# A two-layer decoder trunk: the four-expert round moved from last to fourth, with the overflow branches, two weight tiles and the last rows' parts re-ordered around it

## The chip, the cores and the metric

One core of a Trainium2 chip runs the whole kernel. The metric is device microseconds of one execution. Matmuls run on TensorE (PE, with its weight loads PEld); VectorE is DVE, ScalarE is ACT, GpSimd is POOL, and SyncE (SP) issues nearly all DMAs.

## What is computed

Two layers (DEPTH 2) over 256 tokens of 1024 columns. Each layer is a token mixer (four causal branches behind one input projection), a layer norm, then a mixture of 16 experts of which each token uses two, and a second layer norm:

```python
mix = token_mixer(x, cos, sin, lam_init, w_in[l], ...)
x = layer_norm(DEEPNORM_ALPHA * x + mix, ln1_g[l], ln1_b[l])
ffn = hierarchical_moe(x, w_rg[l], b_rg[l], w_re[l], b_re[l], w_gate[l], w_up[l], w_down[l])
x = layer_norm(DEEPNORM_ALPHA * x + ffn, ln2_g[l], ln2_b[l])
...
hg = jnp.einsum('bsd,edh->bseh', x, w_gate)
hu = jnp.einsum('bsd,edh->bseh', x, w_up)
act = jax.nn.silu(hg) * hu * gate[..., None]
return jnp.einsum('bseh,ehd->bsd', act, w_down)
```

`gate` is zero for the experts that a token does not use. The expert hidden size is 256, everything is float32.

## The kernel before, in words

**Weights come in units of 1 MB** (128 x 2048 float32). A layer has 33 units for the mixer and 48 for the experts: each expert has two units for gate and up (one for each half of the 1024 input columns) and one for down. SP issues one DMA for a unit (`Unit`, L117) as soon as the buffer that it goes to is free; `look(n)` (L448) issues units up to the n-th, in the order of the list `feed`, and `raw(e, j)` (L470) calls it each time that PE code asks for a unit, so the place of a DMA in SP's program follows the PE code with a lead. There are 14 rotating buffers (4 `raw`, 10 `sp`, `CYCLE`) and three more for the first units of the experts: a tile of two (`T16a`, units 8 and 9) and `acc` (unit 10). Below, "unit 38" is the 38th of the 48 in the order of `feed`, counted from 0; 48 to 51 are the first four of the next layer's mixer.

**The experts run in rounds.** A round multiplies the rows of a few experts at once, each in its own strip of PE: six rounds of two experts with 64 slots each, and one round of four experts with 32 slots. Rounds 0 to 2 are experts 0 to 5; the other ten are sorted by their number of tokens at run time, and the four smallest make the four-expert round, which is the last, round 6. In a round p PE does, one after the other and interleaved with the rounds beside it: `gu(p, 0)` and `gu(p, 1)` (L699, gate and up), `turn` (L738, L740, transposes), `down` (L707) and `scatter` (L715, the rows are added to their tokens in PSUM). `residual_mm` (L726) adds the layer's input, whose two parts `hl` ACT and DVE make (`residual_parts`, L719, L720). Matmuls go in order, so a unit that is late stops PE.

**Three branches on the numbers of tokens** stand in the expert part. `most` (L797): if the largest expert has over 64 tokens, three units of it are fetched again (`fetch`, L693, tiles `ow`, `od`) for its overflow. `past` (L852) takes the same condition and computes that overflow beside the last rounds. `rare` (L807): if more than that is needed, a long body with loops. In this run the largest expert has over 64 tokens in layer 1 and not in layer 0, and `rare` is never taken. Each engine has the branches in its own program, SP too, so a DMA that stands behind `rare` there waits until SP is past it. `spare` (L681 on) makes the overflow's slots on DVE and ACT.

**Around them**: the layer norm's rows `gb2` (tile `lnp`, 1 MB, L815) are loaded near the end of the experts; the small rows of the mixer `rw` (L1095) and `bc` (L1096) are loaded once per layer; `ahead` (L845) casts the first units of the next layer's mixer into high and low parts (ACT L134, DVE L138), and `parts_of` splits the last round's rows `y` in the same way (ACT L96, DVE L97) before their scatter.

Of the kernel before, what the change touches and what calls it, by code (L numbers as in the profile page):

```python
# [22 lines left out]
P = 128  # L23
# [12 lines left out]
STAT = 6  # L36
PAIRS = 6
HALF = CAP // 2
NP = PAIRS + 1
SLOTS = NP * 128  # L40
# [29 lines left out]
def trunk(ctx: ExitStack, tc: tile.TileContext, x, xT, wu, rows, brow, lnp, cst, ut, out):  # L70
# [40 lines left out]
    class Unit:  # L111


        def __init__(self, l, i, pieces=1, raw=None, src=None):
            self.raw = raw if raw is not None else raw_p.tile([P, 2048], F32, tag="raw", name=nm("raw"))
            if pieces:
                self.load = nc.sync.dma_start(self.raw, wu[l * NU + i] if src is None else src)  # L117
            self.parts = {}
            self.after = None

# [296 lines left out]
    def tail(l, x_in, mhi, mlo, rw, wg, sw, unit, last):  # L417
# [16 lines left out]
        def places(p):  # L434

            w = CAP if p < PAIRS else HALF
            c, c0 = (0, p * P) if p < STAT // 2 else (1, (p - STAT // 2) * P)
            return [(2 * p + j, slice(j * w, (j + 1) * w), xg[c], slice(c0 + j * w, c0 + (j + 1) * w)) for j in range(P // w)]

        def places_n(p):  # L440
            return [2 * p + j for j in range(2 if p < PAIRS else 4)] if 0 <= p < NP else []

# [5 lines left out]
        def look(n):  # L448
            while len(us) < min(n, limit if place else feed.index((STAT, 0))):
                i = len(us)  # L450
                if i >= len(feed):
                    us.append(Unit(l + 1, i - len(feed), raw=None if i == len(feed) else
                                   sp_p.tile([P, 2048], F32, tag="sp", name=nm("wr"))))
                else:
                    if i == 8:
                        two.append(mp.tile([P, 4096], F32, tag="T16a", name=nm("w2")))
                    if i in (8, 9):
                        r = two[0][:, (i - 8) * 2048:(i - 7) * 2048]
                    elif i == 10:
                        r = big.tile([P, 2048], F32, tag="acc", name=nm("w1"))  # L460
                    else:
                        r = None if (i if i < 8 else i - FIRST) % CYCLE in range(RAW) else sp_p.tile([P, 2048], F32, tag="sp", name=nm("wr"))
                    e, j = feed[i]
                    us.append(Unit(l, FIRST_E + 3 * e + j, raw=r) if e < STAT else Unit(l, None, raw=r, src=place[0](e + 4, j)))
# [59 lines left out]
        def gather(c, k, t, parts=(0, 1)):  # L524
# [24 lines left out]
        with manual():  # L549
# [68 lines left out]
            key = sm.tile([P, 16], F32, tag="key", name=nm("key"))  # L618
            top = sm.tile([P, 20], F32, tag="top", name=nm("top"))
            topi = sm.tile([P, 20], I32, tag="topi", name=nm("topi"))  # L620
            ei = sm.tile([P, 20], I32, tag="ei", name=nm("ei"))

            def counts():

                V.scalar_tensor_tensor(key, cn, 16.0, down15, op0=OP.mult, op1=OP.add)
                V.max(top[:, 10:18], key[:, STAT:])
# [3 lines left out]
                V.tensor_scalar(top[:, 16:20], low[:, 10:14], -1.0, None, op0=OP.mult)  # L630
                V.max(top[:, 0:8], key)
                V.scalar_tensor_tensor(top[:, 8:9], top[:, 0:1], -16.0 * MORE, top[:, 1:2], op0=OP.add, op1=OP.max)
                V.scalar_tensor_tensor(top[:, 8:9], top[:, 19:20], 16.0 * (CAP - HALF), top[:, 8:9], op0=OP.add, op1=OP.max)
                V.tensor_copy(top[:, 9:10], top[:, 8:9])
# [15 lines left out]
            def slot_gates(p0, p1):  # L650
                gp = psumd()[:, :(p1 - p0) * 8].rearrange("p (a b) -> p a b", b=8)
                for p in range(p0, p1):
                    n = len(places_n(p))
                    for t in range(2):
                        T.matmul(gp[:, p - p0, :2 * n], Q[t][:, p * P:(p + 1) * P],
                                 rts[t].gh[:, 2 * p:2 * p + n, :].rearrange("p a b -> p (a b)"), start=(t == 0), stop=(t == 1))
                for a, b, n in ((p0, min(p1, PAIRS), 2), (max(p0, PAIRS), p1, 4)):
                    for j in range(n if a < b else 0):
                        r = slice(j * P // n, (j + 1) * P // n)
                        V.tensor_reduce(gs[r, a:b], gp[r, a - p0:b - p0, 2 * j:2 * j + 2], axis=AX.X, op=OP.add)  # L660

            def order():
# [5 lines left out]
                for t in range(2):  # L668
                    o = sm.tile([P, 2, n], F32, tag="ord", name=nm("ord"))
                    for i, v in enumerate((rts[t].s16, rts[t].g16)):  # L670
                        V.tensor_tensor(m[:, 1], m[:, 0], v[:, None, :].to_broadcast([P, n, 16]), op=OP.mult)
                        V.tensor_reduce(o[:, i], m[:, 1], axis=AX.X, op=OP.add)
                    slots(t, STAT * CAP, o[:, 0, :2 * PAIRS - STAT])
                    slots(t, 2 * PAIRS * CAP, o[:, 0, 2 * PAIRS - STAT:], HALF)
                    finish(rts[t].two(slice(STAT, NE), o[:, 1]))
# [19 lines left out]
            def gu(p, kh, ps):  # L695
                w = [raw(i, kh) for i in places_n(p)]
                for k in range(4):
                    for (_, r, x_, c), w_ in zip(places(p), w):
                        T.matmul(ps[r, :], x_[:, 4 * kh + k, c], w_[:, k * 512:(k + 1) * 512],  # L699
                                 start=(kh == 0 and k == 0), stop=(kh == 1 and k == 3))  # L700

            def down(p, aT, pd, halves=(0, 1)):
                w = [raw(i, 2) for i in places_n(p)]
                for half in halves:
                    for k in range(2):
                        for (_, r, _, _), w_ in zip(places(p), w):
                            T.matmul(pd[half][r, :], aT[:, k, r], w_[:, k * 1024 + half * 512:k * 1024 + (half + 1) * 512],  # L707
# [49 lines left out]
            gu(0, 1, ps)  # L757
            slot_gates(0, STAT // 2)
            si = expert_act(ps, gs[:, 0:1])
# [10 lines left out]
            def pair(p, si, todo, ps=None):  # L770
# [9 lines left out]
                if p == 1:  # L780
                    slot_gates(STAT // 2, NP)
# [4 lines left out]
            for p in range(1, NP - 4):  # L786
                si, todo = pair(p, si, todo)
                if p == 1:
# [63 lines left out]
        with tc.If(most > 16 * CAP + 15, label=f"past{l}") as c:  # L852
            with manual():
                steps.chunk(0, CAP, (lambda: out6(0), lambda: out6(1), lambda: scatter6(0),
                                     lambda: (scatter6(1), turn7()), lambda: (ahead(0), down7((0,)))))
                ahead(1)
                down7((1,))
        with c.Else(), manual():
# [5 lines left out]
            ahead(0)  # L864
            ahead(1)
            down7()
        with manual():
            if last:
                A.activation(gs[:, 0:1], gs[:, 0:1], AF.Square)
            ahead(2)  # L870
            y = mp.tile([P, 2, D], F32, tag="T16a", name=nm("y"))
            y7 = big.tile([P, 2, 2, 512], F32R, tag="xtok", name=nm("y7"))
            yy = [parts_of((ps, tp6)[half], y7[:, half]) for half in range(2)]

# [67 lines left out]
            else:  # L942
# [9 lines left out]
                for half in range(2):  # L952
                    done(1, half)
                nc.sync.dma_start(x2d, y)
        return None if last else (x2d, nhi, nlo, us[len(feed):])

    def overflow(topi, counts, spare, fetch, ww, wd, oo, q, gt, x1, sums):
# [96 lines left out]
        def fours(i):  # L1054

            k_ = nc.values_load(topi[0:1, i:i + 1], min_val=0, max_val=16 * S + 15)
            with tc.If(k_ > 16 * HALF + 15):
                with manual():
                    fetch(i, ww, wd)
                    chunk(i, HALF)  # L1060
                if i > 16:
                    fours(i - 1)

        def rare():

            past(counts[0], 0, CAP + MORE)
            experts(1)
            fours(19)
            with manual():
                spare(0, CAP, q, gt)  # L1070
                fetch(0, ww, wd)

        return SimpleNamespace(chunk=chunk, rare=rare, room=room)

    def layer(l, x_in, thi, tlo, last, early):
# [3 lines left out]
        def unit():  # L1079
# [4 lines left out]
            return Unit(l, i)  # L1084

        lam_init = 0.8 - 0.6 * math.exp(-0.3 * l)
        tks = [slice(0, P), slice(P, 2 * P)]
# [394 lines left out]
```

## Time and profile before

| | |
|---|---|
| median of 3 runs | 687.53 us (686.36 to 689.56) |
| the profiled execution | 687.56 us |
| its span, first to last instruction | 685.8 us |
| mean granted TensorE clock | 0.986 |
| PE busy | 652.8 us (95%) |
| DVE, ACT busy | 412.3 us (60%), 287.0 us (42%) |
| DMA bytes | 185.73 MB, mean 271 GB/s |

The profiled execution stands 0.03 us from the median, and 1.8 us of it lie outside the span. Times in the trace count from the span's start. Layer 0 ends near 342 us, where PE takes up layer 1's input projection; the expert part of layer 1 lies about 335 us behind that of layer 0.

### The profile page before, as it was taken

The page shows a single profiled execution, that of the slowest core. Times are in us where ns is not written, and L with a number is a line of the kernel's source. Part 1 is how long each engine was busy: PE and PEld are TensorE (multiplying, and loading weights), DVE is VectorE, ACT ScalarE, POOL GpSimd, SP SyncE. Part 2 cuts the span into 40 slices and gives each one's busy share as a digit, 9 for nine tenths or more (in the row PEclk, how much of TensorE's full clock was granted, in tenths as well). Part 3 has the DMA queues.
Part 4 walks back from the last instruction along what each step waited for, and adds up shares of the span by engine and source line. Part 5 has one row for each costly group of instructions (what it writes and reads, how often), then busy time and mean ns, then how long its engine had stood idle before and what let it go on. Part 6 is the DMA issues. An engine that isn't in the chain of part 4 may idle for free. (4 is left out here: it accounts for less than half of the span.)

```text
span 685.8 us, 9776 instructions
## 1 busy us (share of the span) xinstructions
PE 652.8 (95%) x3579; PEld 462.3 (67%) x3579; DVE 412.3 (60%) x932; ACT 287.0 (42%) x465; POOL 5.9 (1%) x26
## 2 busy tenths in 40 slices
PE   8999999999999999998699999999999999999983
PEld 5899778888888354333479987888887953543331
DVE  4998667876557832211799875786853677321116
ACT  5755675454224231111455547664441252211122
POOL 0100000000000000000000000000000000000000
PEclk9999999999999999999899999999999999999997
DMA  8995544466759997979927363456566799699871
GB/s 302 369 338 190 206 131 176 172 219 224 289 192 391 410 419 290 396 291 424 421 100 275 123 236 105 152 183 249 182 225 265 271 409 421 261 402 418 318 326 62
DMA packets 28001, 185.73 MB, mean 271 GB/s; under 512 B 3104, under 2 KB 3232, under 8 KB 6432
## 3 DMA queue, kind: packets, MB, share of 16 engines
q1 hardware_dynamic: 27936, 184.94, 70.4%
q8 instruction: 32, 0.52, 0.3%
q14 instruction: 33, 0.27, 0.1%
HBM read 182.83 MB, written 2.10 MB: 270 GB/s over the span
## 5 line engine op out<-in xcount | busy, mean ns | idle before, releaser
L138 DVE TENSOR_TENSOR sp<-raw,sp 128x1024 fp32r<-128x1024 f32 x122 | 147.9, 1221 | 53.7 <-ACT sp L134 43.6
L134 ACT CAST sp<-raw 128x1024 fp32r<-128x1024 f32 x122 | 126.0, 1051 | 105.3 <-PE mm L229 72.5
L229 PE MATMUL mm<-sp,thi 128*128 128x512 f32 (+1 forms) x320 | 96.5, 382 | 1.5 <-ACT sp L96 0.9
L229 PE MATMUL mm<-sp,nhi 128*128 128x512 f32 (+1 forms) x320 | 97.4, 382 | 0.3 <-ACT nhi L96 0.3
L699 PE MATMUL ps<-wr,xg 128*64 128x512 f32 (+1 forms) x352 | 80.0, 596 | 0.0
L229 PEld LDWEIGHTS mm<-sp,thi 128*128 128x128 f32 x320 | 58.9, 188 | 13.5 <-ACT sp L96 1.5
L229 PEld LDWEIGHTS mm<-sp,nhi 128*128 128x128 f32 x320 | 58.8, 188 | 11.7 <-issue 0.5
L229 PE MATMUL mm<-sp,nlo 128*128 128x512 f32 (+1 forms) x160 | 61.4, 385 | 0.5 <-DVE nlo L97 0.4
L229 PE MATMUL mm<-sp,tlo 128*128 128x512 f32 (+1 forms) x160 | 60.1, 380 | 0.0
L699 PEld LDWEIGHTS ps<-wr,xg 128*64 128x64 f32 (+1 forms) x352 | 23.0, 128 | 37.2 <-issue 36.5
L229 PE MATMUL dn<-sp,yhl 128*128 128x512 f32 x192 | 47.8, 392 | 0.0
L409 DVE SCALAR_TENSOR_TENSOR si<-ps,gs,si 128x256 f32<-128x256 f32 x14 | 6.8, 483 | 62.6 <-ACT si L408 62.4
L699 PE MATMUL ps<-raw,xg 128*64 128x512 f32 (+1 forms) x144 | 43.2, 596 | 0.8 <-DVE xg L541 0.8
L229 PE MATMUL mm<-sp,mhl 128*128 128x512 f32 (+1 forms) x192 | 41.0, 368 | 0.9 <-ACT mhl L96 0.5
L229 PEld LDWEIGHTS dn<-sp,yhl 128*128 128x128 f32 x192 | 35.8, 188 | 7.4
L229 PEld LDWEIGHTS mm<-sp,mhl 128*128 128x128 f32 x192 | 32.6, 189 | 7.5 <-DVE mhl L97 1.1
L229 PE MATMUL mm<-thi,sp 128*128 128x256 f32 x192 | 35.6, 286 | 1.4 <-ACT scr L1225 1.3
L229 PE MATMUL mm<-nhi,sp 128*128 128x256 f32 x192 | 35.7, 286 | 0.3 <-ACT misc L1122 0.3
L97 DVE TENSOR_TENSOR yy<-dn,yy 128x512 fp32r<-128x512 f32 x24 | 16.4, 690 | 31.8 <-ACT yy L96 31.8
L229 PEld LDWEIGHTS mm<-sp,nlo 128*128 128x128 f32 x160 | 30.1, 188 | 6.6 <-DVE nlo L97 1.0
L229 PEld LDWEIGHTS mm<-sp,tlo 128*128 128x128 f32 x160 | 30.1, 188 | 5.5
L707 PE MATMUL dn<-wr,aT 128*64 128x512 f32 x112 | 31.5, 613 | 2.2 <-DMA wr<-in_wu_dram 2.2
(305 smaller groups left out, 974.8 us busy)
## 6 DMA issues: line engine op xcount, KB each, us to landing
raw<-in_wu_dram SPq DMA_DIRECT2D x91, 1024.0 KB, 5.2
wr<-in_wu_dram SPq DMA_DIRECT2D x63, 1024.0 KB, 9.5
w<-in_wu_dram SPq DMA_DIRECT2D x6, 1024.0 KB, 14.9
raw<-in_wu_dram SPq DMA_DIRECT2D x8, 256.0 KB, 6.0
lnp<-in_lnp_dram SPq DMA_DIRECT2D x4, 512.0 KB, 6.0
lnp<-in_lnp_dram SPq DMA_DIRECT2D x2, 1024.0 KB, 15.7
ow<-in_wu_dram SPq DMA_DIRECT2D x2, 1024.0 KB, 10.6
xr<-in_xT_dram SPq DMA_DIRECT2D x4, 256.0 KB, 5.8
```

Of the source, the lines that this page charges most:

```text
L97: eng.tensor_tensor(lo, src, f32(hi), op=OP.subtract)
L134: A.copy(self.parts[q][0], self.raw[:, q * 1024:(q + 1) * 1024])
L138: V.tensor_tensor(lo, self.raw[:, q * 1024:(q + 1) * 1024], f32(hi), op=OP.subtract)
L229: T.matmul(ps, a, b, start=(first and i == 0), stop=(last and i == n - 1))
L409: V.scalar_tensor_tensor(si, ps[:, 256:512], gate, si, op0=OP.mult, op1=OP.mult)
L699: T.matmul(ps[r, :], x_[:, 4 * kh + k, c], w_[:, k * 512:(k + 1) * 512], start=(kh == 0 and k == 0), stop=(kh == 1 and k == 3))
L707: T.matmul(pd[half][r, :], aT[:, k, r], w_[:, k * 1024 + half * 512:k * 1024 + (half + 1) * 512], start=(k == 0), stop=(k == 1))
```

## The change

- The four-expert round becomes round 3 (`FOUR`), right behind the three rounds of experts 0 to 5; rounds 4 to 6 are pairs again. `feed`, the sort's columns and the slots follow.
- `rare` is moved ahead of `pair(3)`, with `most` and its `fetch` and `spare` directly behind it. Before, `most` stood there and `rare` one round later.
- The early tile of two units is `T16b` in place of `T16a`, and holds units 6 and 7 in place of 8 and 9; the gathered rows `xg` and the overflow's `ow` change tiles accordingly.
- Layer 1's `rw` and `bc` are issued behind unit 37 of layer 0's experts; before, `bc` was issued early in the kernel and `rw` at the gather.
- `gb2` stands behind units 48 to 51 in SP's program; before, ahead of them.
- In the tail of layer 0, `ahead` casts one half of a unit ahead of `down7`, and the parts of the rows `y` then alternate with the next casts; before, three casts came first.

```diff
-PAIRS = 6
+FOUR = STAT // 2
 HALF = CAP // 2
-NP = PAIRS + 1
+NP = 7
...
-            w = CAP if p < PAIRS else HALF
+            w = HALF if p == FOUR else CAP
...
-                    if i == 8:
-                        two.append(mp.tile([P, 4096], F32, tag="T16a", name=nm("w2")))
-                    if i in (8, 9):
-                        r = two[0][:, (i - 8) * 2048:(i - 7) * 2048]
+                    if i == 6:
+                        two.append(mp.tile([P, 4096], F32, tag="T16b", name=nm("w2")))
+                    if i in (6, 7):
+                        r = two[0][:, (i - 6) * 2048:(i - 5) * 2048]
...
-            look(min(i + FIRST, FIRST + 8) if i < 11 else i + CYCLE)
+
+            look(FIRST + i - max(0, min(i - 6, 2)) - (i > 10))
...
-                xg[c] = mp.tile([P, KD, n], F32, tag="T16b" if c == 0 else "T16a", name=nm("xg"))
+                xg[c] = mp.tile([P, KD, n], F32, tag="T16a" if c == 0 else "T16b", name=nm("xg"))
...
-            spare(0, CAP, fq, fg)
-            ww = mp.tile([P, 4096], F32, tag="T16b", name=nm("ow"))
+            ww = mp.tile([P, 4096], F32, tag="T16a", name=nm("ow"))
             wd = big.tile([P, 2048], F32, tag="thi", name=nm("od"))
-        with tc.If(most > 16 * CAP + 15):
-            fetch(0, ww, wd)
         steps = overflow(topi, (most, rest), spare, fetch, ww, wd, oo, fq, fg, x1, lambda: acc)
-        with manual():
-            hl = residual_parts(0)
-            tc.mark_branch_hint_location(f"rare{l}", rest > 16 * CAP + 15, engines=(mybir.EngineType.PE,))
-            si, todo = pair(NP - 4, si, todo)
-            residual_mm(0, hl)
-            ps = start(NP - 2)
         steps.room(big, "acc")
         with tc.If(rest > 16 * CAP + 15, label=f"rare{l}"):
             steps.rare()
         with manual():
+            spare(0, CAP, fq, fg)
+        with tc.If(most > 16 * CAP + 15):
+            fetch(0, ww, wd)
+        with manual():
+            hl = residual_parts(0)
+            si, todo = pair(NP - 4, si, todo)
+            residual_mm(0, hl)
             hl = residual_parts(1)
-            si, todo = pair(NP - 3, si, todo, ps)
+            si, todo = pair(NP - 3, si, todo)
...
-            ahead(2)
             y = mp.tile([P, 2, D], F32, tag="T16a", name=nm("y"))
             y7 = big.tile([P, 2, 2, 512], F32R, tag="xtok", name=nm("y7"))
-            yy = [parts_of((ps, tp6)[half], y7[:, half]) for half in range(2)]
+            yy = []
+            for half in range(2):
+                yy.append(parts_of((ps, tp6)[half], y7[:, half]))
+                ahead(1 + half)
...
-        with tc.issue_after(early[2].load.ins) if l == 0 else nullcontext():
+        with tc.issue_after(turn_of(early).load.ins):
             nc.sync.dma_start(rw, rows[l])
             nc.sync.dma_start(bc, brow[l].partition_broadcast(P))
```

**SP around `rare`, layer 0.** The rows are SP's program; `wr` and `raw` are buffers of units. Before, the last unit ahead of `rare` is 42:

```order
L117 ISA
L117 DMA wr_2872<-in_wu_dram 128x2048
L117 ISA
L117 DMA wr_2903<-in_wu_dram 128x2048
L117 ISA
L117 DMA wr_2915<-in_wu_dram 128x2048
L807 COMPARE_AND_BRANCH
```

With the change the last unit ahead of `rare` (now L801) is 38, and the next layer's `rw` and `bc` stand before it:

```order
L117 DMA wr_2738<-in_wu_dram 128x2048
L1099 DMA rw_6738<-in_rows_dram 128x956
L1100 DMA bc_6739<-in_brow_dram 128x916
L117 ISA
L117 DMA wr_2750<-in_wu_dram 128x2048
L801 COMPARE_AND_BRANCH
```

The first unit behind `rare` is now 39 in place of 43. PE needs both in its `down` of one round: before, units 42 and 43 were those of round 5,

```order
L707 MATMUL dn_6476<-wr_2915,aT_6417 64x512
L707 MATMUL dn_6476<-wr_6293,aT_6417 64x512
L707 MATMUL dn_6476<-wr_2915,aT_6417 64x512
L707 MATMUL dn_6476<-wr_6293,aT_6417 64x512
L707 MATMUL dn_6496<-wr_2915,aT_6417 64x512
```

and now 38 and 39 are those of round 4:

```order
L708 MATMUL dn_6373<-wr_2750,aT_6346 64x512
L708 MATMUL dn_6373<-wr_6155,aT_6346 64x512
L708 MATMUL dn_6373<-wr_2750,aT_6346 64x512
L708 MATMUL dn_6373<-wr_6155,aT_6346 64x512
L708 MATMUL dn_6374<-wr_2750,aT_6346 64x512
```

So the pair of units between which SP passes `rare` belongs to a `down` one round earlier.

**SP at the end of layer 0's experts.** Before, from unit 47 on (`lnp` is `gb2`, what follows are units 48 to 51):

```order
L117 DMA raw_6388<-in_wu_dram 128x2048
L815 DMA lnp_6375<-in_lnp_dram 128x2048
L117 DMA raw_6390<-in_wu_dram 128x2048
L117 DMA wr_6392<-in_wu_dram 128x2048
L117 DMA wr_6394<-in_wu_dram 128x2048
L117 DMA wr_6429<-in_wu_dram 128x2048
```

and with the change:

```order
L117 DMA raw_6329<-in_wu_dram 128x2048
L117 DMA raw_6331<-in_wu_dram 128x2048
L117 DMA wr_6358<-in_wu_dram 128x2048
L117 DMA wr_6360<-in_wu_dram 128x2048
L117 DMA wr_6375<-in_wu_dram 128x2048
L816 DMA lnp_6398<-in_lnp_dram 128x2048
```

`gb2` went behind four units of the next layer.

**ACT in the tail of layer 0**, from the last copies of the slots on. Before (`sp` are high parts of unit 48 and 49, `y` the high parts of the last rows):

```order
L742 COPY aT_6462<-dn_6614 128x256
L744 CAST QT_6461<-dn_6614 128x256
L134 CAST sp_6453<-raw_6390 128x1024
L134 CAST sp_6455<-raw_6390 128x1024
L852 UNCONDITIONAL_BRANCH
L134 CAST sp_6457<-wr_6392 128x1024
L96 CAST y_6647<-ps_6377 128x512
L96 CAST y_6647<-ps_6412 128x512
```

and with the change:

```order
L743 COPY aT_6449<-dn_6591 128x256
L745 CAST QT_6448<-dn_6591 128x256
L134 CAST sp_6440<-raw_6331 128x1024
L853 UNCONDITIONAL_BRANCH
L96 CAST y_6612<-ps_6400 128x512
L134 CAST sp_6442<-raw_6331 128x1024
L96 CAST y_6612<-ps_6409 128x512
L134 CAST sp_6444<-wr_6358 128x1024
```

The first `y` cast has one cast of the next layer ahead of it in place of three, and the second has two.

## Rows read from the trace of the kernel before

**Rows 1.** What PE waited for, whole span: total us, times, longest us.
```profile
PE mm L715 <- ACT y L96: 5.5, 1, 5.5
PE dn L707 <- DMA wr<-in_wu_dram: 2.2, 1, 2.2
...
PE ps L707 <- DMA raw<-in_wu_dram: 1.3, 1, 1.3
```

**Rows 2.** Busy time by 5 us: PE, PEld, DVE, ACT, POOL, granted clock, DMA share, GB/s.
```profile
330.00:335.00 5.00, 2.56 (x5) 1.78 (x6) 4.40 (x7) 3.91 (x5) 0.00 (x0) 0.50 1.01 421
335.00:340.00 5.00, 5.00 (x21) 3.99 (x21) 4.76 (x16) 0.42 (x1) 0.00 (x0) 0.88 1.02 424
650.00:655.00 5.00, 2.81 (x7) 0.60 (x7) 0.00 (x0) 0.33 (x1) 0.00 (x0) 0.86 0.99 416
655.00:660.00 5.00, 4.18 (x18) 1.50 (x16) 1.18 (x3) 0.96 (x2) 0.00 (x0) 0.80 0.99 419
```

**Rows 3.** What SP's queue waited for in the experts, 240 to 345, then 590 to 672 us.
```profile
SPq L807 <- SPq L807: 12.3, 3, 5.6
...
SPq L797 <- SPq L797: 0.2, 1, 0.2
...
SPq L807 <- SPq L807: 18.9, 7, 5.1
```

**Rows 4.** SP's DMA issues in order of time, layer 1: start us, us, count.
```profile
597.90 3.77 SPq L117 DMA_DIRECT2D wr<-in_wu_dram  x3
...
615.10 33.96 SPq L117 DMA_DIRECT2D wr<-in_wu_dram  x10
648.13 0.93 SPq L117 DMA_DIRECT2D wr<-in_wu_dram  x2
```

**Rows 5.** Issue to landing of the units issued at 628.38, 648.13 and 615.10 us.
```profile
DMA to landing us min/median/max: 19.3/19.3/19.3
...
DMA to landing us min/median/max: 4.9/4.9/4.9
...
DMA to landing us min/median/max: 14.5/14.5/14.5
```

**Rows 6.** PE in order of time, layer 1: round 4's `down`, then round 5's.
```profile
634.72 3.60 PE L707 MATMUL dn<-raw,aT 128*64 128x512 f32 x16
...
653.08 3.18 PE L707 MATMUL dn<-wr,aT 128*64 128x512 f32 x6 [2.19 <-DMA wr<-in_wu_dram]
...
658.60 1.94 PE L707 MATMUL dn<-wr,aT 128*64 128x512 f32 x8
```

**Rows 7.** SP's DMA issues in order of time, layer 0.
```profile
262.80 3.77 SPq L117 DMA_DIRECT2D wr<-in_wu_dram  x3
...
276.81 30.80 SPq L117 DMA_DIRECT2D wr<-in_wu_dram  x10
...
309.56 0.37 SPq L815 DMA_DIRECT2D lnp<-in_lnp_dram  x1
```

**Rows 8.** PE in order of time, layer 0: round 4's `down`, then the layer's last rows.
```profile
299.63 3.60 PE L707 MATMUL dn<-raw,aT 128*64 128x512 f32 x16
...
331.86 0.79 PE L715 MATMUL mm<-y,QT 128*128 128x512 f32 x1 [5.47 <-ACT y L96]
```

**Rows 9.** ACT in order of time, tail of layer 0.
```profile
330.28 1.04 ACT L134 CAST sp<-wr 128x1024 fp32r<-128x1024 f32 x1 [0.52 <-DMA wr<-in_wu_dram]
331.23 1.07 ACT L96 CAST y<-ps 128x512 fp32r<-128x512 f32 x2
```

**Rows 10.** DVE in order of time, tail of layer 0.
```profile
336.67 0.75 DVE L295 SCALAR_TENSOR_TENSOR y<-mm,nmv,lnp 128x512 f32<-128x512 f32 x1
```

**Rows 11.** DMA issues, 309.5 to 309.7 us: KB each, us from issue to landing.
```profile
lnp<-in_lnp_dram SPq DMA_DIRECT2D x1, 1024.0 KB, 15.7
```

**Rows 12.** What ACT waited for, whole span: total us, times, longest us.
```profile
ACT hl L719 <- DVEq L807: 12.5, 2, 6.3
```

**Rows 13.** What SP's queue waited for, 255 to 270 us.
```profile
SPq L117 <- PE dn L707: 3.1, 1, 3.1
```

More of the change, by code (lines that the diff above doesn't have):

```diff
@@ L118, in __init__ @@
             self.parts = {}
-            self.after = None
+            self.after = self.before = None
         def quarter(self, q):
@@ L434, in places @@
         def places(p):
-            w = CAP if p < PAIRS else HALF
-            c, c0 = (0, p * P) if p < STAT // 2 else (1, (p - STAT // 2) * P)
-            return [(2 * p + j, slice(j * w, (j + 1) * w), xg[c], slice(c0 + j * w, c0 + (j + 1) * w)) for j in range(P // w)]
+            w = HALF if p == FOUR else CAP
+            c, c0 = (0, p * P) if p < FOUR else (1, (p - FOUR) * P)
+            return [(slice(j * w, (j + 1) * w), xg[c], slice(c0 + j * w, c0 + (j + 1) * w)) for j in range(P // w)]
         def places_n(p):
-            return [2 * p + j for j in range(2 if p < PAIRS else 4)] if 0 <= p < NP else []
+            a = 2 * p + 2 * (p > FOUR)
+            return list(range(a, a + (4 if p == FOUR else 2))) if 0 <= p < NP else []
         feed = [f_ for p in range(NP + 1) for f_ in [(i, j) for j in range(2) for i in places_n(p)] + [(i, 2) for i in places_n(p - 1)]]
@@ L461, in look @@
                     else:
-                        r = None if (i if i < 8 else i - FIRST) % CYCLE in range(RAW) else sp_p.tile([P, 2048], F32, tag="sp", name=nm("wr"))
+                        r = None if (i if i < 6 else i - FIRST) % CYCLE in range(RAW) else sp_p.tile([P, 2048], F32, tag="sp", name=nm("wr"))
                     e, j = feed[i]
@@ L618, in tail @@
             key = sm.tile([P, 16], F32, tag="key", name=nm("key"))
-            top = sm.tile([P, 20], F32, tag="top", name=nm("top"))
-            topi = sm.tile([P, 20], I32, tag="topi", name=nm("topi"))
-            ei = sm.tile([P, 20], I32, tag="ei", name=nm("ei"))
+            top = sm.tile([P, 22], F32, tag="top", name=nm("top"))
+            topi = sm.tile([P, 22], I32, tag="topi", name=nm("topi"))
+            ei = sm.tile([P, 22], I32, tag="ei", name=nm("ei"))
             def counts():
                 V.scalar_tensor_tensor(key, cn, 16.0, down15, op0=OP.mult, op1=OP.add)
-                V.max(top[:, 10:18], key[:, STAT:])
+                V.max(top[:, 14:22], key[:, STAT:])
                 low = sm.tile([P, 18], F32, tag="low", name=nm("low"))
@@ L629, in counts @@
                 V.max(low[:, 10:18], low[:, 0:10])
-                V.tensor_scalar(top[:, 16:20], low[:, 10:14], -1.0, None, op0=OP.mult)
+                V.tensor_scalar(top[:, 10:14], low[:, 10:14], -1.0, None, op0=OP.mult)
                 V.max(top[:, 0:8], key)
                 V.scalar_tensor_tensor(top[:, 8:9], top[:, 0:1], -16.0 * MORE, top[:, 1:2], op0=OP.add, op1=OP.max)
-                V.scalar_tensor_tensor(top[:, 8:9], top[:, 19:20], 16.0 * (CAP - HALF), top[:, 8:9], op0=OP.add, op1=OP.max)
+                V.scalar_tensor_tensor(top[:, 8:9], top[:, 13:14], 16.0 * (CAP - HALF), top[:, 8:9], op0=OP.add, op1=OP.max)
                 V.tensor_copy(top[:, 9:10], top[:, 8:9])
@@ L652, in slot_gates @@
                 for p in range(p0, p1):
-                    n = len(places_n(p))
+                    e = places_n(p)
                     for t in range(2):
[L655 to L659, printed above, removed]
+                        T.matmul(gp[:, p - p0, :2 * len(e)], Q[t][:, p * P:(p + 1) * P],
+                                 rts[t].gh[:, e[0]:e[-1] + 1, :].rearrange("p a b -> p (a b)"), start=(t == 0), stop=(t == 1))
+                for a, b in ((0, FOUR), (FOUR, FOUR + 1), (FOUR + 1, NP)):
+                    for j, (r, _, _) in enumerate(places(a) if p0 <= a < p1 else ()):
                         V.tensor_reduce(gs[r, a:b], gp[r, a - p0:b - p0, 2 * j:2 * j + 2], axis=AX.X, op=OP.add)
@@ L697, in gu @@
                 for k in range(4):
-                    for (_, r, x_, c), w_ in zip(places(p), w):
+                    for (r, x_, c), w_ in zip(places(p), w):
                         T.matmul(ps[r, :], x_[:, 4 * kh + k, c], w_[:, k * 512:(k + 1) * 512],
@@ L705, in down @@
                     for k in range(2):
-                        for (_, r, _, _), w_ in zip(places(p), w):
+                        for (r, _, _), w_ in zip(places(p), w):
                             T.matmul(pd[half][r, :], aT[:, k, r], w_[:, k * 1024 + half * 512:k * 1024 + (half + 1) * 512],
@@ L757, in tail @@
             gu(0, 1, ps)
-            slot_gates(0, STAT // 2)
+            slot_gates(0, FOUR)
             si = expert_act(ps, gs[:, 0:1])
@@ L780, in pair @@
                 if p == 1:
-                    slot_gates(STAT // 2, NP)
+                    slot_gates(FOUR, NP)
                 return si, out_(p, qt, aT)
@@ L786, in tail @@
             for p in range(1, NP - 4):
+                if p == NP - 5:
+                    tc.mark_branch_hint_location(f"rare{l}", rest > 16 * CAP + 15, engines=(mybir.EngineType.PE,))
                 si, todo = pair(p, si, todo)
@@ L864, in tail @@
             ahead(0)
-            ahead(1)
             down7()
@@ L954, in tail @@
                 nc.sync.dma_start(x2d, y)
+            us[-1].before = us[36]
         return None if last else (x2d, nhi, nlo, us[len(feed):])
@@ L1060, in fours @@
                     chunk(i, HALF)
-                if i > 16:
+                if i > 10:
                     fours(i - 1)
         def rare():
+            fetch(0, ww, wd)
             past(counts[0], 0, CAP + MORE)
             experts(1)
[L1068 to L1071, printed above, removed]
+            fours(13)
         return SimpleNamespace(chunk=chunk, rare=rare, room=room)
@@ L1084, in unit, with turn_of @@
             return Unit(l, i)
+        def turn_of(early):
+            return early[-1].before or early[-1]
         lam_init = 0.8 - 0.6 * math.exp(-0.3 * l)
```

5 lines of the change are left out of this document (2 added, 3 removed).

## The prediction

> **What bounds the kernel now.** I read the busy shares first, then what PE waited for, then the stretches around its two longest waits, and last SP's program, since both waits end in a DMA. PE is busy for 652.8 of 685.8 us and executes in order, so a change pays only where PE stands or where its clock is down. In the whole span three waits are longer than 1.3 us [rows 1]: 5.5 us at the end of layer 0, where the scatter of the last rows waits for their cast on ACT; 2.2 us in round 5's `down` of layer 1 and 1.3 us in the last `down` of layer 0, both for a unit of weights. The granted clock shows what follows [rows 2]: 1.00 while PE is busy, then 0.50 and 0.88 behind the wait of 5.5 us, 0.86 and 0.80 behind that of 2.2 us. 0.50 is the lower level, 1.2 GHz of 2.4.
>
> Both waits for units lie behind `rare`, which is not taken. SP's own queue says why [rows 3]. At L807 it waits on itself for 12.3 us in layer 0 and for 18.9 us in layer 1; at the short branch L797 0.2 us. In these waits it goes through the DMAs in flight one by one, and it issues nothing until the last has landed. Layer 1 shows it whole: the unit issued at 628.38 lands 19.3 us later, at 647.7; the next issue is at 648.13 [rows 4] and lands 4.9 us after that, at 653.03 [rows 5]. PE needed it at about 650.9 and goes on at 653.08 [rows 6]. A **drain** thus costs the stream 653.0 - 647.7 = 5.3 us between two landings. With the queue full a unit lands every 2.49 us (1.05 MB at 421 GB/s, the rate of [rows 2]), so 2.8 us of transfers are lost, and whatever stands first behind `rare` comes after all that was in flight.
>
> **The change part by part.** *Layer 1: `rare` one `down` earlier.* The unit in front of `rare` is now 38, the one behind it 39, and round 4's `down` needs both at 634.72 [rows 6]. When does 38 land? The unit that lands first behind the gather, 28 in both kernels, is issued at 597.90 [rows 4] and lands 4.9 us later, 602.8. Ten more at 2.49 us give 627.7 as the lower end. The tenth megabyte behind it in the trace, three of them the overflow's units, was issued at 615.10 and landed 14.5 us later, 629.6 [rows 5], with the pauses that buffers made: the upper end. I take 628.5. After the drain comes not 39 but the overflow of this layer, since `fetch` now stands directly behind `rare`: its first unit lands at 628.5 + 5.3 = 633.8, two more at 2.49 us, then 39: 641.3, and with 0.2 us for the short branch [rows 3] and 0.3 us for the fetch's register loads (my allowance) 641.8. PE would stand for 641.8 - 634.7 = **+7.1 us**, between 6.1 and 8.0 by the two ends.
>
> PE then starts at a low clock. Six matmuls behind the wait of 2.19 us took 3.18 us; at the pace of the later eight, 1.94 us, they would take 1.46, so 1.7 us were lost there [rows 6]. Behind the wait of 5.5 us the two stretches of [rows 2] fall short of 1.00 by 0.50 and 0.12, of which PE was busy for 2.6 and 5.0 us: 1.3 + 0.6 = 1.9 us. The new wait is longer: I take **+2.1**, from 1.7 to 2.6. In return before's wait and its slow matmuls go, **-2.2 and -1.7**: behind the stop PE runs nine microseconds later than before while the units go on at 2.49 us, four to a round that takes about 11 us. Layer 1: 7.1 + 2.1 - 2.2 - 1.7 = **+5.3**, from +3.9 to +6.7.
>
> *Layer 0: the same drain, no overflow.* Unit 28 is issued at 262.80 [rows 7] and lands at 267.7; ten units later, with `rw` and `bc` (0.94 MB, 2.3 us) between, 38 is there at 294.9, and 39 at 294.9 + 5.3 + 0.2 = 300.4, or 301.4 with one pause for a buffer. PE needs it at 299.63 [rows 8]: a wait of 0.8 to 1.8 us, **+1.3**. It stands in place of the 1.3 us that the last `down` waited [rows 1], **-1.3**, for by then the stream is ahead: 47 lands eight units after 39, near 320.8.
>
> *The tail of layer 0.* Before, the `y` cast starts at 331.23 behind a cast that itself waited for unit 49 [rows 9], and PE stands from 326.4 to 331.86 [rows 8]. Now one cast is ahead of it, of unit 48, which lands at about 323.3; the `y` cast can start when PE has written its rows, at 326.5, and the rest follows some 4.5 us earlier than before on PE, ACT and DVE. But `gb2` is late instead: the first scaling by it is at 336.67 [rows 10]; before, `gb2` had landed at 309.56 + 15.7 = 325.2 [rows 7, 11], now it stands five megabytes behind unit 47: 320.8 + 5 x 2.49 = 333.3, or 334.7 if the buffer pauses of before return. So the gain is cut from about 4 us to 336.67 - 333.6 = **-3.0**, from -2.0 to -3.9 (the last if `gb2` were in time). Between the end of the rows and `gb2` PE has only its 14 filler matmuls. Layer 0 together: **-2.8** with 0.2 us for the later start, from -1.2 to -4.
>
> *ACT and DVE at the new place.* The skip held ACT for 6.2 us in each layer before it made `hl` (12.5 us in two) [rows 12]. It now comes one round earlier with `spare` behind it; the first thing that PE needs from ACT there is the activation of the next round, some 3 us after ACT would be back. I cost it at nothing; if that cover is gone, up to 2 us in each layer. The Trainium skill ("Runtime: NRT & Kernel Launch", Instruction fetch mechanics) says that a taken branch whose target is not in the resident window has to fetch it by DMA before execution continues, a rule that speaks against putting the skip where more loads are queued. The trace agrees with it so far, 6.2 us at the long skip against 0.2 at the short one.
>
> *The early tile and `bc`.* Two units start a few microseconds earlier at the front of the experts. But SP stops again at the gather: its issue at 262.80 was released by PE's `down`, which freed a buffer [rows 13], and that is where it was. I cost the head start at nothing. The four-expert round itself costs PE the same in any place: its strips run side by side.
>
> Sum: 687.56 + 5.3 - 2.8 = 690.1, which I round to **690.0 us**; the median of before is 0.03 us from the execution that I count from.
>
> **The rivals.** *A, faster: the head start survives.* If the two early units keep their 5 us past the gather, 38 lands at 623.5 in layer 1, 39 at 636.8, PE stands for 2.1 us as before, and layer 0's wait of 1.3 us is gone as well: 687.5 - 2.8 - 1.3 = 683.4. It decides at 38 landing before about 624. For it: there are two more buffers in use early. Against: the release at 262.80 is by PE, not by a transfer.
>
> *B, slower still: both layers lose.* Pauses for buffers put 38 at the upper end or behind it, PE stands for 8 us or more in layer 1 (+8.0 + 2.6 - 3.9 = +6.7), and in layer 0 `gb2` lands after 336.7, so that nothing is gained there: 694.3. It decides where `gb2` lands. For it: in the trace the tenth megabyte behind unit 28 did come 1.9 us later than ten times 2.49 us allow [rows 5].
>
> *C, the skip is slower with more loads in flight.* If ACT and DVE came back 5 us later than 6.2 us after the branch, PE would wait for the next activation by 3 us in each layer: 696. Against: SP's waits of 12.3 and 18.9 us say that the queues at L807 differed between the layers [rows 3], and ACT waited the same in both. The rule of the Trainium skill above would work in this way.
>
> *D, it does not do what it says.* If `rare` still came behind unit 42 on SP, layer 1 would stay and the tail's gain alone would count: 684.8. The order of SP's program speaks against it.
>
> **How the numbers follow.** The forecast has 0.60, A 0.15, B 0.18, C 0.04, D 0.03. The forecast's own range is 687 to 693 (687.56 + 3.9 - 4 to 687.56 + 6.7 - 1.2). With part of A and of B on either side the range is 685.0 to 694.0. A difference of 0.5%, 3.4 us, is about what a measurement of this kernel can tell from none: below 684.1 faster, above 691.0 slower. The forecast lies mostly inside: of its 0.60, 0.36 are within the bound and 0.24 above; A counts 0.12 faster and 0.03 same, B and C slower, D same. Faster 0.13, same 0.42, slower 0.45.
>
> **What would show it.** In the changed profile: SP's queue waiting on itself at L801 in both layers and no DMA issued meanwhile; in layer 1 a wait of some 7 us of round 4's `down` (L708) for a `wr` unit near 634.7, with the overflow's units landing ahead of it, and a granted clock well below 1.00 behind it; no wait in round 5's `down`. In layer 0 a wait near 1.3 us at 299.6, the `y` cast before 328, the first scaling near 333.6 and released by the `lnp` load, layer 1's first matmul some 3 us earlier. The prediction is wrong if 39 lands in time in layer 1, if SP passes L801 without a drain, or if PE waits for ACT or DVE behind the skip.

## The result and the profile after

The changed kernel takes 697.01 us (median of 4 runs, 695.14 to 697.59), the kernel before in the same runs 687.2 us (686.36 to 689.56). The ratio is 1.0132, 95% interval 1.0100 to 1.0165: slower, by 9.8 us where 2.4 were forecast, and outside the stated range. The profiled execution took 697.59 us, its span is 695.5 us, the mean granted clock 0.982.

What PE waited for, whole span of the changed kernel (total us, times, longest us); it answers to [rows 1]:

```profile
PE dn L708 <- DMA wr<-in_wu_dram: 9.0, 2, 7.2
PE ps L256 <- DVE y L298: 2.7, 1, 2.7
...
PE mm L716 <- PEq L801: 1.4, 2, 0.7
```

The wait of 5.5 us for the `y` cast is gone; the tail's new order alone leaves 2.95 us of it (sixth experiment). In its place stand a wait of 7.2 us in layer 1's round 4 and a new one of 2.7 us at the end of layer 0, where PE's transposes wait for the vector engine's last step of the norm.

SP's queue at the branch in both layers, 240 to 345 us and then 590 to 672 us, answering to [rows 3]:

```profile
SPq L801 <- SPq L801: 17.4, 4, 7.5
...
SPq L805 <- SPq L805: 0.4, 1, 0.4
...
SPq L801 <- SPq L801: 17.6, 6, 5.4
```

The drain is there in both layers. On the path past the skipped body SP waits for nine semaphores, one after the other. In layer 1 the first passes 5.4 us behind the branch, the last at 629.5, when unit 38, issued at 611.27, has landed:

```profile
L801 SPq EVENT_SEMAPHORE  x9: 17/17/17, 617.1 to 629.5; - x9
...
DMA to landing us min/median/max: 18.2/18.2/18.2
```

SP's issues of layer 1 in order of time (start us, us, count) show what follows it:

```profile
608.25 3.36 SPq L117 DMA_DIRECT2D wr<-in_wu_dram  x4
630.79 1.67 SPq L694 DMA_DIRECT2D ow<-in_wu_dram  x2
633.69 0.34 SPq L694 DMA_DIRECT2D od<-in_wu_dram  x1
634.47 3.55 SPq L117 DMA_DIRECT2D wr<-in_wu_dram  x6
```

Unit 38 is the last of the four of 608.25. Then SP issues nothing for nineteen microseconds, the overflow's three units come next, and unit 39 is issued at 634.47. It landed 9.6 us later, at 644.0:

```profile
wr<-in_wu_dram SPq DMA_DIRECT2D x1, 1024.0 KB, 9.6
```

PE at that place, in order of time, answering to [rows 6]:

```profile
635.82 1.02 PE L708 MATMUL dn<-wr,aT 128*64 128x512 f32 x2
644.08 6.32 PE L708 MATMUL dn<-wr,aT 128*64 128x512 f32 x14 [7.24 <-DMA wr<-in_wu_dram]
650.33 0.97 PE L727 MATMUL mm<-hl,idr 128*128 128x512 f32 x3
```

Two matmuls can begin without unit 39, fourteen wait. Those fourteen then take 6.3 us, where sixteen took 3.6 before [rows 6]. The granted clock says why (stretches of 5 us, columns as in [rows 2]):

```profile
640.00:645.00 5.00, 0.92 (x4) 0.30 (x6) 0.00 (x0) 0.00 (x0) 0.00 (x0) 0.50 1.00 423
645.00:650.00 5.00, 5.00 (x14) 1.40 (x10) 0.69 (x1) 0.58 (x1) 0.00 (x0) 0.55 1.01 423
```

0.50 and 0.55 are the lower of the two levels for nearly all of these ten microseconds. And the end of layer 0 (DVE's first scaling by `gb2`, then PE's transposes), answering to [rows 10]:

```profile
336.82 0.75 DVE L295 SCALAR_TENSOR_TENSOR y<-mm,nmv,lnp 128x512 f32<-128x512 f32 x1 [1.91 <-DMA lnp<-in_lnp_dram]
...
339.81 1.29 PE L256 MATMUL ps<-cs,y 128*128 128x128 f32 x8 [2.72 <-DVE y L298]
```

`gb2` (`lnp`) is now what ends the layer, and it lands no earlier than the old chain arrived: the scaling was at 336.67 before [rows 10].

### The profile page after: what moved, and what is told of

Read it like the earlier page. It is cut to its first block, busy times and chain, and to the rows that moved or that the text cites. A ratio compares the mean times of both kernels' runs of the same rounds, so it can differ in the third digit from the quotient of the medians.

```text
span 695.5 us, 9804 instructions
## 1 busy us (share of the span) xinstructions
PE 658.1 (95%) x3579; PEld 464.1 (67%) x3579; DVE 412.7 (59%) x932; ACT 286.6 (41%) x465; POOL 6.1 (1%) x26
## 5 line engine op out<-in xcount | busy, mean ns | idle before, releaser
L708 PE MATMUL dn<-wr,aT 128*64 128x512 f32 (+1 forms) x160 | 50.3, 644 | 9.0 <-DMA wr<-in_wu_dram 9.0
L700 PEld LDWEIGHTS ps<-wr,xg 128*64 128x64 f32 (+1 forms) x320 | 24.4, 131 | 32.8 <-issue 30.9
L708 PEld LDWEIGHTS dn<-wr,aT 128*64 128x64 f32 (+1 forms) x160 | 13.6, 142 | 38.2 <-issue 27.3
L700 PE MATMUL ps<-raw,xg 128*64 128x512 f32 (+1 forms) x144 | 36.0, 596 | 0.8 <-DVE xg L543 0.8
L96 ACT CAST yy<-dn 128x512 fp32r<-128x512 f32 x24 | 14.1, 585 | 51.7 <-PE dn L708 47.1
## 6 DMA issues: line engine op xcount, KB each, us to landing
lnp<-in_lnp_dram SPq DMA_DIRECT2D x2, 1024.0 KB, 17.7
```

The costliest lines, as they stand in the source:

```text
L96: A.copy(hi, src)
```

## The experiments

The kernels were timed in groups, each on one chip with runs of the kernel before beside them, and the medians of before differ by up to 1.6 us between the chips. Differences below are therefore against the median of before in the same group: 688.82 us for the first four, 688.05 for the next four, 687.61 for the last two. On that count the changed kernel stands at +9.8.

**M** is the theory that the place of the drain, with the overflow behind it, makes unit 39 late and that the stream's lead decides the end of layer 0. **R** is its rival: that the earlier skip, or the order of the rounds itself, costs the time.

### The rare branch put back alone

```diff
-        with tc.If(rest > 16 * CAP + 15, label=f"rare{l}"):
-            steps.rare()
         with manual():
             spare(0, CAP, fq, fg)
         with tc.If(most > 16 * CAP + 15):
             fetch(0, ww, wd)
         with manual():
             hl = residual_parts(0)
             si, todo = pair(NP - 4, si, todo)
             residual_mm(0, hl)
+            ps = start(NP - 2)
+        with tc.If(rest > 16 * CAP + 15, label=f"rare{l}"):
+            steps.rare()
+        with manual():
             hl = residual_parts(1)
-            si, todo = pair(NP - 3, si, todo)
+            si, todo = pair(NP - 3, si, todo, ps)
```

The end of `rare`'s body is the old one again, too, and the hint for PE stands one round later.

> The changed kernel with the rare branch alone put back one round later on every engine (SP now passes it behind unit 47 instead of 38); the overflow's fetch stays between units 38 and 39. Theory M (SP's drain at the branch plus the three fetched units make unit 39 late in layer 1, the low clock follows): 39 lands 4 units after 38, about 639.4, so round 4's down waits some 3.6 us instead of 7.2 and loses about 2 us to the clock instead of 3.1: 697.0 - 4.7 = about 692. Rival R (the place of the skip on PE, ACT and DVE, or the round order itself, costs the time): at most the 0.5 us per layer that the earlier skip cost on PE comes back, 696.

686.99 us, -1.8 (ratio 0.9977, 0.9958 to 0.9997): the loss is gone whole. Round 4's `down` in layer 1:

```profile
632.64 1.02 PE L708 MATMUL dn<-wr,aT 128*64 128x512 f32 x2
636.69 3.65 PE L708 MATMUL dn<-wr,aT 128*64 128x512 f32 x14 [3.03 <-DMA wr<-in_wu_dram]
```

The wait is 3.0 us, about the 3.6 that M gave, but the fourteen matmuls behind it run at full pace, where I had put 2 us, and layer 0 gained some 3 us that I had put at nothing: without the drain ahead of 39, its two waits for units in rounds 4 and 5 go as well. R's blame of the order of the rounds falls: the four-expert round is fourth here too. In the changed kernel PE waits 1.4 us at L801 in two layers, where it waited 0.6 at L807 before; the next experiment shows that this is not the earlier place of the skip.

### The overflow's fetch one round later, the branch left early

```diff
         with manual():
             spare(0, CAP, fq, fg)
-        with tc.If(most > 16 * CAP + 15):
-            fetch(0, ww, wd)
-        with manual():
             hl = residual_parts(0)
             si, todo = pair(NP - 4, si, todo)
             residual_mm(0, hl)
+        with tc.If(most > 16 * CAP + 15):
+            fetch(0, ww, wd)
+        with manual():
             hl = residual_parts(1)
```

> The changed kernel with the fetch of the overflow's three units moved one round later (behind unit 46 in SP's program); the rare branch stays early, before unit 39. M: 39 lands straight after the drain, about 636, where PE needs it; round 4's down waits under 1 us, no low clock there: 697.0 - 7.2 - 3.1 + 0.5 = about 687. R: the branch has not moved, so 696 to 697.

685.35 us, -3.5 (0.9948, 0.9932 to 0.9964). Round 4's `down` in layer 1 is whole again:

```profile
634.72 3.60 PE L708 MATMUL dn<-wr,aT 128*64 128x512 f32 x16
```

PE's wait at the skip, as early as in the changed kernel, is what it was before, so the other 0.8 us of the changed kernel go with the second branch directly behind it:

```profile
PE mm L716 <- PEq L801: 0.6, 2, 0.3
```

So neither the early branch nor the early fetch alone makes the kernel slower than before. It is the two behind one another: the drain, then 3 MB, and only then the unit that PE waits for. This is the experiment that settles the sign of the change.

### `gb2` ahead of units 48 to 51 again

Units 48 to 51 are issued behind `gb2`'s DMA (`look` does not go on to them before; that line is not shown):

```diff
-            nc.sync.dma_start(gb2, lnp[l, 2:4].partition_broadcast(P))
+            loaded.append(nc.sync.dma_start(gb2, lnp[l, 2:4].partition_broadcast(P)))
...
-                    us.append(Unit(l + 1, i - len(feed), raw=None if i == len(feed) else
-                                   sp_p.tile([P, 2048], F32, tag="sp", name=nm("wr"))))
+                    with tc.issue_after(loaded[0].ins):
+                        us.append(Unit(l + 1, i - len(feed), raw=None if i == len(feed) else
+                                       sp_p.tile([P, 2048], F32, tag="sp", name=nm("wr"))))
```

> The changed kernel with the layer norm's rows gb2 issued ahead of units 48 to 51 again. M (gb2's landing at 336.6 ends layer 0): it lands about 327, the transposes of layer 0's rows start about 337 instead of 339.8, PE's idle 2.7 us and most of the 1.6 us of low clock behind it go: 697.0 - 3.5 = about 693.5. R (layer 0's end is held by the casts and the vector chain): 696 to 697, transposes still near 339.

696.56 us, +7.7 (1.0112, 1.0092 to 1.0133), which is not told apart from the changed kernel: 6.3 to 9.2 us above before, against 6.9 to 11.3. A miss for M as I had put it. ACT and DVE in the tail of layer 0:

```profile
328.91 1.04 ACT L134 CAST sp<-raw 128x1024 fp32r<-128x1024 f32 x1 [3.32 <-DMA raw<-in_wu_dram]
329.87 0.58 ACT L96 CAST y<-ps 128x512 fp32r<-128x512 f32 x1
...
337.07 0.75 DVE L295 SCALAR_TENSOR_TENSOR y<-mm,nmv,lnp 128x512 f32<-128x512 f32 x1
```

`gb2` is no longer waited for, but unit 48 is one megabyte later, its cast stands on ACT ahead of the `y` cast, and the chain reaches the scaling at 337.07 by itself; the transposes start at 340.58, later than the 339.81 of the changed kernel. Two landings hold this tail, 48's and `gb2`'s, and swapping them trades one for the other.

### Filler matmuls in the wait

```diff
                 pd = [psumd(), psumd()]
+                if last and p == NP - 3:
+                    keep_warm(Q[0], 30, pd[1])
                 down(p, aT, pd)
```

> The changed kernel with 30 matmuls that compute nothing used, on PE ahead of round 4's down in layer 1, so that PE is busy during the wait for unit 39. If the slow matmuls behind the wait are the clock's answer to idleness: down's 14 matmuls take 3.2 us instead of 6.3, 697.0 - 3.1 = about 694. If they are paced by the landing units or by operands: no change, 697.

693.92 us, +5.1 (1.0075, 1.0054 to 1.0096). PE in layer 1, with the filler (L549):

```profile
635.20 7.12 PE L549 MATMUL dn<-Q,idr 128*128 128x512 f32 x30
642.24 1.07 PE L708 MATMUL dn<-wr,aT 128*64 128x512 f32 x2
644.14 3.65 PE L708 MATMUL dn<-wr,aT 128*64 128x512 f32 x14 [0.82 <-DMA wr<-in_wu_dram]
```

PE goes on 0.06 us from when it did, so unit 39 came at the same time, and the fourteen matmuls take 3.65 in place of 6.32 us. These 2.7 us are the price of the clock behind this wait, shown by itself: the matmuls were not paced by operands. The granted clock of the three stretches from 635 to 650 is 1.00. Between the two medians lie 3.1 us, and 4.7 when each is counted against before on its own chip, so the times alone do not give the price.

### `rw` and `bc` where they were

```diff
-        with tc.issue_after(turn_of(early).load.ins):
+        with tc.issue_after(early[2].load.ins) if l == 0 else nullcontext():
```

> The changed kernel with the next layer's rows rw and bc issued where they were before (bc early in the kernel, rw at the gather), so that 0.94 MB less stand ahead of unit 38 in layer 0. M (the stream's lead sets layer 0): 38 to 51 and gb2 land 2.7 us earlier there, round 4's and round 5's downs wait 0 in place of 1.7 and 0.8 us, gb2 lands near 334 and layer 0's transposes start near 337.5; layer 1 unchanged: 697.0 - 2.5 = about 694.5. R (casts and the vector chain hold the end of layer 0): transposes start no earlier than 339, 696 to 697.

693.82 us, +5.8 (1.0091, 1.0060 to 1.0121). Layer 0's waits, 220 to 345 us:

```profile
PE ps L256 <- DVE y L298: 2.7, 1, 2.7
PE mm L716 <- DVE y L97: 0.9, 1, 0.9
PE dn L708 <- DMA raw<-in_wu_dram: 0.7, 1, 0.7
PE mm L716 <- PEq L801: 0.6, 1, 0.6
```

The whole stream of layer 0 is 2.7 us earlier, round 4's wait of 1.7 us is gone, the scaling by `gb2` still waits for its landing (it starts at 334.10), and all of layer 0 ends 2.6 us or more earlier. The 0.94 MB ahead of the drain cost somewhat more than the 2.3 us that they take to transfer at 421 GB/s. Round 5 still waits 0.7 us, which I had put at 0.

### The tail's order alone, in the kernel before

```diff
             ahead(0)
-            ahead(1)
             down7()
...
-            ahead(2)
...
-            yy = [parts_of((ps, tp6)[half], y7[:, half]) for half in range(2)]
+            yy = []
+            for half in range(2):
+                yy.append(parts_of((ps, tp6)[half], y7[:, half]))
+                ahead(1 + half)
```

> The kernel of before with the tail's new order alone (one cast ahead of down7, the parts of y alternating with the casts), nothing moved on SP. If this order is what shortens layer 0's end: the first y cast starts near 329 instead of 331.2 (it waits for unit 48's cast only), gb2 is long there, so the transposes start 2 us or more earlier: about 685. If DVE's chain of casts, statistics and norm holds the end whatever the order: 687, transposes near 340.

686.53 us, -1.5 (0.9980, 0.9962 to 0.9997): a small gain, between the two expectations. The `y` cast starts at 328.13 where it had been 331.23 [rows 9], and the scaling at 335.20 in place of 336.67 [rows 10]. But PE (order of time):

```profile
334.17 1.91 PE L715 MATMUL mm<-y,QT 128*128 128x512 f32 x4
335.88 4.26 PE L547 MATMUL dn<-Q,idr 128*128 128x512 f32 x14
339.98 1.04 PE L256 MATMUL ps<-cs,y 128*128 128x128 f32 x8
```

Four scatter matmuls take 1.91 us that take 1.09 in the changed kernel, and the 14 filler matmuls 4.26 in place of 3.38: the clock is granted at 0.60 and 0.72 in the two stretches from 330 to 340, behind a wait of 2.95 us for `y`. The transposes come when the filler ends, 0.5 us earlier than before. The cast order took 3 us off its chain, and the low clock and the filler gave most of it back.

### Both stream costs out

The edits of the fetch and of `rw` and `bc` together.

> The changed kernel with the overflow's fetch one round later and rw and bc where they were before: both stream costs taken out. M: e2's 685.4 less the 2.5 us of e5: about 683. R: 685.

682.63 us, -5.4 (0.9918, 0.9897 to 0.9939). No wait for a unit is left in round 4 of either layer. The first scaling by `gb2` is at 333.45 and still waits 2.0 us for it.

### The rare branch earlier still

On top of the later fetch, `rare` goes between `pair(1)` and `pair(2)`; the loads of the two counts and the hint go ahead of `pair(1)`:

```diff
+            most = nc.values_load(topi[0:1, 0:1], min_val=0, max_val=16 * S + 15)
+            rest = nc.values_load(topi[0:1, 8:9], min_val=-16 * MORE, max_val=16 * S + 15)
+            tc.mark_branch_hint_location(f"rare{l}", rest > 16 * CAP + 15, engines=(mybir.EngineType.PE,))
+            si, todo = pair(1, si, todo)
...
         with manual():
+            si, todo = pair(2, si, todo)
             spare(0, CAP, fq, fg)
```

> e2 with the rare branch one round earlier still, behind unit 28, where SP waits for PE to free a buffer and little is in flight. M (the drain's price is what is in flight plus the lead of the units behind it): SP's wait at the branch is some 5 us instead of 19, the next unit lands by 274, round 4's down in layer 0 waits 0 instead of 1.3 us and none appears elsewhere: about 684. Rival (the skip itself holds ACT, DVE or PE): a new wait of PE for ACT or DVE behind the branch of 2 to 5 us per layer, 689 or more.

684.07 us, -4.0 (0.9934, 0.9914 to 0.9955). SP's queue in layer 0, then PE's waits for the skip (255 to 345 us):

```profile
SPq L806 <- SPq L806: 6.9, 2, 6.8
...
SPq L798 <- SPq L798: 5.4, 1, 5.4
```

```profile
PE dn L708 <- DVEq L798: 0.9, 1, 0.9
...
PE mm L716 <- PEq L798: 0.3, 1, 0.3
```

With one load in flight SP's wait at the skip is 5.4 us in place of 17.4, near the 5 that M gave. That load landed at 264.8, and SP is past the skip at 265.7, so most of these 5.4 us had a landing to wait for. But in the changed kernel, with the queue full, the first of SP's waits at the skip was 5.4 us long too, so this part seems not to depend on what is in flight. The Trainium skill ("Runtime: NRT & Kernel Launch", Instruction fetch mechanics) has a cause for such a stall, without a length: a taken branch out of the resident window fetches its target by DMA before execution goes on. The profile has one transfer of the kind "instruction" in this wait, which fits, but it does not say for which engine (260.3 to 265.7 us: number, MB, share):

```profile
q14 instruction: 1, 0.01, 0.4%
```

The rival is there as well, but small: PE waits 0.9 us for DVE behind the skip in layer 0, and 1.7 us at the skip in layer 1.

At the later fetch (L806) SP now waits 6.9 us, where the same short branch cost 0.2 in [rows 3]. On this path SP waits for four semaphores in place of nine. They pass from 299.4 to 306.3 us, and a unit issued at 288.44 lands 17.7 us later, at 306.1:

```profile
L806 SPq EVENT_SEMAPHORE  x4: 17/17/17, 299.4 to 306.3; - x4
...
DMA to landing us min/median/max: 17.7/17.7/17.7
```

So the short branch can make SP wait for landings as well, and its price changes with its place. PE did not wait for it: its waits above name no unit.

### `gb2` between units 49 and 50

The edit of `gb2` above, on top of the kernel with both stream costs out, with units 48 and 49 left ahead of it.

> e7 with gb2 issued between units 49 and 50 instead of behind 51. In e7 the first scaling by gb2 waits 2.0 us for its landing at 333.2, while 48 and 49 are there for their casts long before. If both conditions of the tail hold together (48 and 49 ahead of the y parts, gb2 ahead of the scaling): gb2 lands near 328.3, the first scaling starts near 331.5 instead of 333.45, layer 0 ends 2.0 us earlier: 682.6 - 2.0 = about 680.6. If units 50 and 51 are then late for the casts behind the norm: 682 to 683.

680.15 us, -7.5 (0.9887, 0.9865 to 0.9909). The first scaling:

```profile
331.58 0.75 DVE L295 SCALAR_TENSOR_TENSOR y<-mm,nmv,lnp 128x512 f32<-128x512 f32 x1
```

It waits for nothing, 1.9 us earlier than with `gb2` behind 51, and PE's wait at the transposes falls from 2.8 to 0.9 us. The clock behind it stays at 1.00 (330 to 345 us). This version beats both kernels.

### The same with the branch behind unit 28

The two moves of the last two edits together, with `rw` and `bc` in their old places.

> e10 with the rare branch behind unit 28 as in e9. In e7 no PE wait for a unit is left in round 4, so the earlier branch has nothing to take away, while in e9 it added a wait of PE of 1.7 us at the branch and 0.9 us for DVE behind it: e10's time or up to 1.5 us more, 680.6 to 682. If the stream's lead still counted, 1 us less than e10.

680.78 us, -6.8 (0.9897, 0.9876 to 0.9918), as expected: the intervals overlap, nothing is gained, and PE waits 2.0 us at the skip (L800) in two layers.

## Why the prediction was wrong

**The mechanism and the sign of layer 1 were right.** SP drains at the skip, the overflow comes next, unit 39 is late, PE stands in round 4's `down` and goes on at the lower clock; the first, second and fourth experiments take this away part by part. Three terms around it were mis-sized or misread:
- *The wait*, forecast 7.1. The 7.24 us of the profile look right, but two matmuls ran ahead of them. From its arrival at 635.82 PE was held until 644.08, 8.3 us: PE came 1.1 us later than before (634.72 in [rows 6]) and unit 39 2.2 us later than forecast (644.0 against 641.8). Unit 38 landed at 629.5, where I took 628.5.
- *The clock behind it*, forecast +2.1 (1.7 to 2.6). Fourteen matmuls took 6.32 us; behind a wait but at the full clock they take 3.65 (first and fourth experiment), so this is **+2.7**. The term was near, but its source was misread: before's six matmuls behind the wait of 2.19 us [rows 6] lost not 1.7 but some 1.3 us, since the same six, behind 2.21 us in the sixth experiment, take 1.93 us at the full clock and not 1.46.
- *The skip on PE, ACT and DVE*, forecast 0: PE waited 0.7 us at it in each layer in place of 0.3, for the fetch's branch directly behind it (second experiment).

Counted on the program, the residual behind this `down` starts at 650.33 in place of 638.25 (PE of before, layer 1, below): 12.1 us, of which 1.1 were there already, so the wait and the clock are 11.0 and not 9.2.

```profile
638.25 1.20 PE L726 MATMUL mm<-hl,idr 128*128 128x512 f32 x4
```

What before's own wait and slow matmuls gave back was 3.9 in the forecast and 4.3 in the trace. Layer 1 so has +6.7 in place of +5.3, the upper end that I had given.

**Layer 0 was wrong**, and this is the step that failed: "the gain is cut from about 4 us to -3.0", because `gb2` would land at 333.3. It landed at 336.6, the bound of rival B (336.7). The stream was later than I summed: 38 at 296.7 for 294.9, which I had summed without a pause, the interval across the drain 6.3 us for 5.5, and behind it one landing that came 1.3 us late, though its unit had been issued 12.0 us earlier. Rounds 4 and 5 waited 1.7 and 0.8 us for units, where I had put one wait of 1.3. The transposes came 0.6 us earlier than before, not 3. And the clock fell behind the new wait of 2.7 us, which I had put at nothing: it is 0.73 from 340 to 345, and the second set of transposes starts 1.0 us later than before. These are PE of before and of the changed kernel, then the stretch of the changed kernel:

```profile
348.24 1.29 PE L256 MATMUL ps<-cs,y 128*128 128x128 f32 x8
...
349.19 1.04 PE L256 MATMUL ps<-cs,y 128*128 128x128 f32 x8
...
340.00:345.00 5.00, 4.53 (x17) 3.23 (x16) 4.86 (x14) 4.43 (x6) 0.00 (x0) 0.73 0.91 380
```

So in the profiled execution layer 0 cost 1.0 us where -2.8 was forecast. The parenthesis that the gain would be 3.9 if `gb2` were in time failed as well: the third experiment puts it in time and gains nothing that can be told apart, for then unit 48 is late for its cast ahead of `y`.

**A stretch of low clock** comes on top in the profiled execution: 0.66 from 665 to 670, where eight matmuls of round 5 took 3.4 us in place of 1.9. It is not in the traces of the first five experiments, and it is in that of the branch behind unit 28 (0.66 from 655 to 660). It is some 1.6 us that differ from one execution to the next; what sets it off was not tried.

So rival B, with 0.18 and 694.3, was nearest: its +6.7 for layer 1 is what the trace shows, and its nothing for layer 0 is 1.0 us short; most of the rest is the late stretch. The stated range ended at 694.0, just below B's own number. In the prediction's arithmetic the two ends of the wait come to 6.3 and 8.2, not 6.1 and 8.0, and the parts of the chances to 0.12 faster and 0.46 slower, not 0.13 and 0.45; neither changes the outcome. Rival A fell at the point where the prediction put it: unit 28 was issued at 262.62 in place of 262.80 [rows 7], so the head start of the early tile was lost at the gather. Rival C fell: the skip cost PE tenths, not 3 us, with more loads queued. D fell with SP's order: 39 is the first of the list's units that is issued behind the skip.

## What to carry to other kernels

An untaken branch is not free on the queue that issues loads: here SP waited for nine semaphores at the long body and four at the short one, each until the load in flight on it had landed, and the price was paid by the first loads behind it. So count what stands between such a branch and the first unit that the bounding engine needs, and move the optional loads behind that unit: moving three of them was worth some 12 us (spans of 695.5 and 683.6). A tail that is held by several landings gains only when all of them are in time, so order the loads by when each is used (48 and 49, `gb2`, then 50 and 51), not group by group.

## What the runs showed of the hardware that was not expected

The low clock behind a wait does not follow from the wait's length alone. The same six matmuls took 3.18 us behind 2.19 us [rows 6] and 1.93 us behind 2.21 us. Fourteen took 3.65 us behind 3.03 us (first experiment), 6.32 behind 7.24, and 5.51 and 5.96 behind two other waits as long. These are the six in the sixth experiment, then the fourteen in the third and the fifth:

```profile
652.81 1.93 PE L707 MATMUL dn<-wr,aT 128*64 128x512 f32 x6 [2.21 <-DMA wr<-in_wu_dram]
...
644.56 5.51 PE L710 MATMUL dn<-wr,aT 128*64 128x512 f32 x14 [7.82 <-DMA wr<-in_wu_dram]
...
640.74 5.96 PE L708 MATMUL dn<-wr,aT 128*64 128x512 f32 x14 [7.07 <-DMA wr<-in_wu_dram]
```

And filler matmuls are themselves on PE's path when the clock is low: 14 of them took 4.26 us in place of 3.38 and held the transposes.
